# A decoder layer's second feed-forward block: one more seven-product pair per gate and up unit, its column sums loaded instead of added

## The chip, the cores and the metric

The kernel runs on one core of one Trainium2 chip. The metric is device time in microseconds (us) of one execution, the median of several runs. A core has five engines with instruction queues of their own: TensorE (PE) multiplies, VectorE (DVE) and ScalarE (ACT) do element-wise work, GpSimd (POOL) and SyncE (SP) here mostly issue DMAs. Engines wait for each other by semaphores alone, and each works through its own queue in order.

## The reference

One decoder layer on 272 tokens (16 learned meta tokens and 256 real ones) of width 2048, all in float32: a SwiGLU feed-forward block, a mixer (attention and a short convolution, each gated), and a second feed-forward block, all with RMS norms. What matters here is the second block, on the 256 real tokens alone, and the mixer's gates:

```python
D_FF = ((8 * D_MODEL // 3 + 255) // 256) * 256        # 5632

def swiglu_ffn(h, w_gu, w_down):
    gate, up = jnp.split(h @ w_gu, 2, axis=-1)
    return (jax.nn.silu(gate) * up) @ w_down
...
        gates = jax.nn.sigmoid(h @ w_gate[layer]).reshape(Bsz, L, N_BRANCH, D_MODEL)
        merged = jnp.sum(gates * z, axis=2)
        s = s + merged @ w_out[layer]

        h = rms_norm(s, norm_ffn2[layer])
        s = s + 0.5 * swiglu_ffn(h, ffn2_w_gu[layer], ffn2_w_down[layer])
    s = rms_norm(s, norm_final)
    return s[:, N_META:]
```

## The kernel before, in words

**Splitting.** Every float32 weight is used as a high part `wh` (ACT rounds it, L381) and a low part `wl = w - wh` (DVE, L382), activations likewise. A product of two numbers then takes three matmuls: high by high, low by high, high by low (L488 to L490). `parts` (L374) makes `wh` and `wl` of one block of weights, 128 rows by two times 512 columns, into rings of three buffers each. `step` (L239) collects what PE shall do with a block and holds it back until two later blocks are split (`AHEAD`).

**Units.** The gate and up weights of the second block are 11 units of 512 gate and 512 up columns (`thirds`, L975: units 0 to 3, 4 to 7, 8 to 10, each run of units followed by its share of the down projection). Unit 0 goes through `linear_tok`; units 1 to 10 through `gate_up_mix` (L578). The mixer's gates are four more such units (L902). In `linear_mix` (L470) a unit's 2048 rows of weights are eight pairs, a pair being two chunks of 128 rows, and `KINDS` says how each pair is multiplied. Rows in two chunks, tokens in two halves of 128 and columns in gate and up make a 2 by 2 by 2 block product. A pair of kind D multiplies it in eight products of 128x128 by 128x512. A pair of kind S takes seven (Winograd's form): it needs four sums of blocks of activations (made once, L455 to L465) and four sums of blocks of weights, made anew for each pair and unit by DVE (`tt`, L514 to L517: one add of 128x1024, then two of 128x512). An S pair is split in four blocks: one single block of 128x512 (product 3) and three double ones (1 and 2; 6 and 4; 5 and 7). Call the blocks n0 to n3, and a D pair's n0 and n1.

**Buffers.** Loaded weights (`st`) and the sums (`tt`) share a ring of five 8 KB buffers (`ST_BUFS`). The pool "a" has 27 buffers for activations and the like (`N_ACT`).

**End of a unit.** Products are summed in eight PSUM banks. When a bank's last product is done, `done` (L548) brings it into the sums `cgate` and `cup` on ACT and DVE; then comes SiLU on ACT (L582), `up * gate` on DVE (L583), and PE transposes the result in two goes of four (`back`, L589, called from `later` in L498 at pair 2 of the next unit).

**Order.** The framework's scheduler puts each engine's queue in an order of its own when the kernel is built; `issue_after` pins an instruction behind another. SP issues weight loads, POOL issues only eight small loads at the start and two for the last norm.

Of the kernel before, what the change touches and what calls it, by code (L numbers as in the profile page):

```python
# [9 lines left out]
F32 = mybir.dt.float32  # L10
# [5 lines left out]
P = 128  # L16
# [15 lines left out]
W_BUFS = 3  # L32
ST_BUFS = 5
LB = 2
N_ACT = 27
EVICT_AT = 1
# [3 lines left out]
LATER_AT = (4, 6)  # L40
KINDS = "DDDSDSDS"
AHEAD = 2
# [3 lines left out]
def decoder_layer(ctx: ExitStack, tc: tile.TileContext, t, out):  # L46
# [3 lines left out]
    wpool = ctx.enter_context(tc.tile_pool(name="w", bufs=W_BUFS))  # L50
    apool = ctx.enter_context(tc.tile_pool(name="a", bufs=N_ACT))
    tmp = ctx.enter_context(tc.tile_pool(name="tmp", bufs=2))
    psum = ctx.enter_context(tc.tile_pool(name="ps", bufs=8, space=bass.MemoryType.PSUM))
# [184 lines left out]

    def step(use):  # L239

        ahead.append(use)
        drain(AHEAD)

    def drain(n=0):
        while len(ahead) > n:
            ahead.pop(0)()

# [66 lines left out]
    def linear_tok(ops, chunks, k0, name, evict, side_at=(5, 9, 13), hold=0, after=None):  # L314
# [46 lines left out]
        for b, c in enumerate(chunks):  # L361
# [10 lines left out]
            step(lambda b=b, wh=wh, wl=wl: use(b, wh, wl))  # L372

    def parts(src, n=2, held=False):  # L374
# [6 lines left out]
        nc.scalar.copy(out=wh, in_=src)  # L381
        nc.vector.tensor_sub(wl, src, wh.bitcast(F32))  # L382
        return wh, wl
# [46 lines left out]
    class Mixed:  # L430

        def __init__(self, norm, g0):
            self.act, self.sums = Act("hn", 0, SEQ), {}
            self.norm, self.g0 = norm, g0
# [12 lines left out]
        def pair(self, p, f):  # L449
# [4 lines left out]
            nc.vector.tensor_sub(tl[:, :, 1, :], f, tl[:, :, 0, :].bitcast(F32))  # L454
            if KINDS[p] == "S":  # L455
# [5 lines left out]
                nc.vector.tensor_add(q[:, 3, :], a12, q[:, 1, :])  # L461
                sp = apool.tile([P, 4, 2, P], F32R, tag="act", name=f"sp{p}")
                nc.scalar.copy(out=sp[:, :, 0, :], in_=q)
                nc.vector.tensor_sub(sp[:, :, 1, :], q, sp[:, :, 0, :].bitcast(F32))
                self.sums[p] = [[sp[:, k, lo, :] for lo in range(2)] for k in range(4)]  # L465
# [3 lines left out]

    def linear_mix(a, w, cols, name, done):  # L470

# [5 lines left out]

        nd, ns = KINDS.count("D"), KINDS.count("S")
        left = {k: 2 * nd * (k in "234x") + ns * (k != "x") for k in "1234567x"}
# [14 lines left out]
        def use(p, n, products):  # L494

            for k, left_op, wh, wl in products:
                product(k, left_op, wh, wl)
            if p == 2 and later:  # L498
                later.pop(0)()
            if n == (1 if KINDS[p] == "D" else 3):  # L500
                if p == 0:
# [4 lines left out]
        def load(p):  # L506
# [3 lines left out]
            for q in range(2):  # L510
                nc.sync.dma_start(out=st[:, :, q, :], in_=rows[:, :, cols[q] : cols[q] + GW])
            if KINDS[p] == "D":
                return st, None
            tt = wpool.tile([P, 4, GW], F32, tag="st", bufs=ST_BUFS, name="tt")  # L514
            nc.vector.tensor_add(tt[:, 0:2, :], st[:, 0, :, :], st.rearrange("p c q f -> p q c f")[:, 1, :, :])
            nc.vector.tensor_add(tt[:, 2, :], tt[:, 0, :], st[:, 1, 1, :])
            nc.vector.tensor_add(tt[:, 3, :], tt[:, 2, :], st[:, 1, 0, :])  # L517
            return st, tt

        loaded = {0: load(0)}  # L520
        for p, kind in enumerate(KINDS):
            st, tt = loaded[p]
            (a11, a21), (a12, a22) = ([a.block(2 * p + c, i) for i in range(2)] for c in range(2))
# [5 lines left out]
            else:  # L529
# [3 lines left out]
                    (st[:, :, 0, :], (("1", a11, 0), ("2", a12, 1))),  # L533
                    (tt[:, 2:4, :], (("6", s2, 0), ("4", a22, 1))),
                    (tt[:, 0:2, :], (("5", s1, 0), ("7", s3, 1))),
# [8 lines left out]
    def mixed(a, w, cols, name, end):  # L544

# [29 lines left out]

        linear_mix(a, w, cols, name, done)

    def gate_up_mix(a, w_gu, g, m, gi):  # L578
# [7 lines left out]

        mixed(a, w_gu, (g * GW, F + g * GW), "pg", end)

# [254 lines left out]
    yc = Act("yc", NH, SEQ)  # L843
    hg = Mixed(norm2, G_MIX)
    for g in range(2):
# [120 lines left out]
    w_gu, w_down = t["ffn2_w_gu"][0], t["ffn2_w_down"][0]  # L966
    hn = Mixed(norm3, G_FFN2)

# [76 lines left out]
```

## Time and profile before

| what | us |
| --- | --- |
| median of 3 runs (lowest, highest) | 2201.43 (2201.15, 2201.85) |
| the profiled execution: time | 2201.99 |
| the profiled execution: span, first to last instruction | 2200.2 |
| first feed-forward block and mixer, to the last product of `o` | about 1476 |
| second block: unit 0 | 1476 to 1522 |
| second block: units 1 to 10 and the down projections | 1522 to 2200 |

The page tells each engine's busy time, DMA's share in 40 slices, the chain of work that ended last, and groups of instructions by line and operands. The timeline lists single instructions; the windows view sums up a stretch of time. A row's duration is start to end of one instruction; consecutive rows of one engine overlap, so how fast an engine gets on is read from the distance of their starts. A row of PE's weight loads (PEld) belongs to the matmul behind it.

### The profile page before, as it was taken

Reading aid. Unit: us, or ns where it says so; the run is one execution under the profiler, and the core shown is the slowest. Engines: PE = TensorE matmul, PEld = TensorE weight load, DVE = VectorE, ACT = ScalarE, POOL = GpSimd, SP = SyncE. Lnnn points to the kernel's source line nnn. Section 1 sums busy time; section 2 is a strip of 40 time slices with the busy share of each in tenths; the row PEclk is TensorE's granted clock in tenths of the full one; section 3 lists DMA queues with packets and bytes.
Section 4 is the critical chain, followed back from the end, with each engine's and each line's share of the span. In section 5 each row is a group of like instructions: output and inputs, shape, how many; then the busy total and the mean of one; then the engine's idle time right before and its main releaser. Section 6 shows DMA issues by size and latency. Waiting matters only on the chain.

```text
span 2200.2 us, 33207 instructions
## 1 busy us (share of the span) xinstructions
PE 2186.4 (99%) x13534; PEld 1973.3 (90%) x13534; DVE 1467.6 (67%) x1904; ACT 1041.6 (47%) x1301; POOL 6.4 (0%) x17
## 2 busy tenths in 40 slices
PE   9999999999999999999999999999999999999998
PEld 8999999999999999898988888888888888888886
DVE  8555554445555565667897777678886688856985
ACT  6443343334333443444555555455554455534554
POOL 0000000000000000000000000000000000000000
PEclk9999999999999999999999999999999999999999
DMA  7545555555545555444445656554566455665562
GB/s 269 177 173 173 173 173 176 180 178 175 173 172 173 173 176 187 154 138 151 165 153 200 211 193 215 185 187 142 193 224 210 155 201 202 227 211 174 190 229 96
DMA packets 192394, 401.97 MB, mean 183 GB/s; under 512 B 8692, under 2 KB 8880, under 8 KB 192240
## 3 DMA queue, kind: packets, MB, share of 16 engines
q1 hardware_dynamic: 191232, 397.97, 53.1%
q8 instruction: 106, 1.74, 0.3%
q0 software_dynamic: 544, 1.21, 0.2%
q10 hardware_dynamic: 464, 0.66, 0.1%
q14 instruction: 48, 0.39, 0.1%
HBM read 397.71 MB, written 2.10 MB: 182 GB/s over the span
## 4 chain that ended last, share of the span: by engine, by line
PE 98%; DVE 1%; ACT 1%; DMA 0%; issue 0%; SPq 0%; DVEq 0%; ACTq 0%
PE pg L490 5%; PE pg L488 5%; PE pg L489 5%; PE pd L289 4%; PE pu L289 4%; PE pd L287 4%; PE pu L287 4%; PE pu L288 4%; PE pd L288 4%; PE pg L289 4%; PE pg L287 4%; PE pg L288 4%; PE pd L329 4%; PE pd L328 4%; PE pd L327 4%; PE o L285 3%
## 5 line engine op out<-in xcount | busy, mean ns | idle before, releaser
L276 DVE TENSOR_TENSOR wl<-st,wh 128x1024 fp32r<-128x1024 f32 x392 | 478.9, 1224 | 453.5 <-ACT wh L275 452.8
L275 ACT CAST wh<-st 128x1024 fp32r<-128x1024 f32 x392 | 411.3, 1050 | 609.9 <-PE pd L288 146.9
L381 ACT CAST wh<-st 128x1024 fp32r<-128x1024 f32 (+1 forms) x360 | 358.5, 1004 | 366.3 <-PE pd L328 113.8
L382 DVE TENSOR_TENSOR wl<-st,wh 128x1024 fp32r<-128x1024 f32 (+1 forms) x360 | 414.2, 1158 | 130.4 <-ACT wh L381 129.9
L287 PE MATMUL pg<-h,wh 128*128 128x272 f32 x704 | 202.9, 289 | 0.9 <-ACT wh L275 0.8
L287 PE MATMUL pu<-h,wh 128*128 128x272 f32 x704 | 203.1, 289 | 0.0
L289 PE MATMUL pd<-m,wl 128*128 128x272 f32 x704 | 203.0, 288 | 0.0
L289 PE MATMUL pu<-h,wl 128*128 128x272 f32 x704 | 203.0, 288 | 0.0
L287 PE MATMUL pd<-m,wh 128*128 128x272 f32 x704 | 202.9, 288 | 0.0
L288 PE MATMUL pu<-h,wh 128*128 128x272 f32 x704 | 202.4, 288 | 0.0
L288 PE MATMUL pd<-m,wh 128*128 128x272 f32 x704 | 202.4, 287 | 0.0
L288 PE MATMUL pg<-h,wh 128*128 128x272 f32 x704 | 201.7, 287 | 0.0
L289 PE MATMUL pg<-h,wl 128*128 128x272 f32 x704 | 200.6, 289 | 0.9 <-DVE wl L276 0.9
L488 PE MATMUL pg<-wh,hn 128*128 128x512 f32 x390 | 152.7, 391 | 0.0
L489 PE MATMUL pg<-wh,hn 128*128 128x512 f32 x390 | 152.0, 390 | 0.0
L490 PE MATMUL pg<-wl,hn 128*128 128x512 f32 x390 | 151.8, 392 | 0.2 <-DVE wl L382 0.2
L327 PE MATMUL pd<-wh,m 128*128 128x512 f32 x352 | 137.5, 391 | 0.0
L328 PE MATMUL pd<-wh,m 128*128 128x512 f32 x352 | 137.0, 389 | 0.0
L329 PE MATMUL pd<-wl,m 128*128 128x512 f32 x352 | 136.9, 390 | 0.0
L382 DVE TENSOR_TENSOR wl<-tt,wh 128x1024 fp32r<-128x1024 f32 x84 | 101.3, 1222 | 52.8 <-ACT wh L381 42.8
L287 PEld LDWEIGHTS pg<-h,wh 128*128 128x128 f32 x704 | 132.3, 188 | 1.5 <-ACT wh L275 1.5
L288 PEld LDWEIGHTS pg<-h,wh 128*128 128x128 f32 x704 | 132.8, 189 | 0.0
(303 smaller groups left out, 4725.4 us busy)
## 6 DMA issues: line engine op xcount, KB each, us to landing
st<-in_ffn_w_gu_dram SPq DMA_DIRECT2D x184, 512.0 KB, 4.4
st<-in_ffn_w_down_dram SPq DMA_DIRECT2D x88, 1024.0 KB, 5.1
st<-in_ffn_w_gu_dram SPq DMA_DIRECT2D x84, 1024.0 KB, 4.9
st<-in_w_in_dram SPq DMA_DIRECT2D x48, 1024.0 KB, 5.1
st<-in_w_gate_dram SPq DMA_DIRECT2D x64, 512.0 KB, 4.4
st<-in_w_branch_dram SPq DMA_DIRECT2D x32, 512.0 KB, 4.7
st<-in_w_out_dram SPq DMA_DIRECT2D x16, 1024.0 KB, 5.0
xin<-in_x_dram SPq DMA_DIRECT2D x8, 256.0 KB, 8.4
```

The costliest lines, as they stand in the source:

```text
L275: nc.scalar.copy(out=wh[:, :m, :], in_=sw)
L276: nc.vector.tensor_sub(wl[:, :m, :], sw, wh[:, :m, :].bitcast(F32))
L287: nc.tensor.matmul(a, wh[:, i, f], act.part(c, 0, t0, t1), start=first, stop=False)
L288: nc.tensor.matmul(a, wh[:, i, f], act.part(c, 1, t0, t1), start=False, stop=False)
L289: nc.tensor.matmul(a, wl[:, i, f], act.part(c, 0, t0, t1), start=False, stop=last)
L327: nc.tensor.matmul(ps, hi, wh[:, q, :], start=first, stop=False)
L328: nc.tensor.matmul(ps, lo, wh[:, q, :], start=False, stop=False)
L381: nc.scalar.copy(out=wh, in_=src)
L382: nc.vector.tensor_sub(wl, src, wh.bitcast(F32))
L488: nc.tensor.matmul(ps[k], hi, wh, start=first, stop=False)
L489: nc.tensor.matmul(ps[k], lo, wh, start=False, stop=False)
L490: nc.tensor.matmul(ps[k], hi, wl, start=False, stop=left[k] == 0)
```

## The change

`KINDS` becomes two tables. The gates keep their three S pairs (`DDDSDSDS`); the units of the second block get `DDSDSSDS`, four S pairs and four D pairs, so 180 matmuls in place of 183. The transposes of the previous unit are called from pair 1 in place of pair 2 there (`TURN_FFN2`).

In the second block the first two sums of an S pair (`t13`) are no longer added by DVE: POOL issues two DMAs per pair, a plain load and one that adds into what the first wrote, into a pool "aux" of three buffers that takes three buffers from pool "a" and that holds the gates' activation sums before. They are issued up to four pairs ahead. The other two sums (`t24`) stay on DVE, pinned behind the split of a given block (`SUMS_*`). `st` and sums have rings of their own (four buffers of `st`, two of 4 KB for sums), and `st` is loaded two pairs ahead. The single block n0 is split into two 2 KB buffers of pool "tmp" and no longer counts in `AHEAD`.

```diff
-ST_BUFS = 5
+ST_BUFS = 4
-N_ACT = 27
+N_ACT = 24
+N_AUX = 3
-KINDS = "DDDSDSDS"
+KINDS_GATES = "DDDSDSDS"
+KINDS_FFN2 = "DDSDSSDS"
+TURN_GATES = 2
+TURN_FFN2 = 1
+SUMS_GATES = {(2, 1): 3, (4, 1): 5, (6, 1): 7}
+SUMS_FFN2 = {(1, 1): 2, (3, 0): 4, (3, 1): 5, (6, 0): 7}
...
-    def step(use):
-        ahead.append(use)
-        drain(AHEAD)
+    def step(use, ring=True):
+        ahead.append((use, ring))
+        while sum(r for _, r in ahead) > AHEAD:
+            ahead.pop(0)[0]()
...
         wh, wl = (
-            (apool.tile([P, 2, GW], F32R, tag="act", name=nm) if held else wpool.tile([P, 2, GW], F32R, tag=nm, name=nm))
+            tmp.tile([P, 1, GW], F32R, tag="sc", name=nm) if n == 1
+            else (apool.tile([P, 2, GW], F32R, tag="act", name=nm) if held else wpool.tile([P, 2, GW], F32R, tag=nm, name=nm))
...
-                sp = apool.tile([P, 4, 2, P], F32R, tag="act", name=f"sp{p}")
+                sp = (aux if self.in_aux else apool).tile([P, 4, 2, P], F32R, tag="act", name=f"sp{p}")
...
-            if p == 2 and later:
+            if p == a.turn_at and later:
                 later.pop(0)()
...
-            tt = wpool.tile([P, 4, GW], F32, tag="st", bufs=ST_BUFS, name="tt")
-            nc.vector.tensor_add(tt[:, 0:2, :], st[:, 0, :, :], st.rearrange("p c q f -> p q c f")[:, 1, :, :])
-            nc.vector.tensor_add(tt[:, 2, :], tt[:, 0, :], st[:, 1, 1, :])
-            nc.vector.tensor_add(tt[:, 3, :], tt[:, 2, :], st[:, 1, 0, :])
-            return st, tt
+            t13 = t24 = None
+            if kinds[p] == "S":
+                if not fetch:
+                    t13 = wpool.tile([P, 2, GW], F32, tag="tt", bufs=2, name="t13")
+                    nc.vector.tensor_add(t13, st[:, 0, :, :], st.rearrange("p c q f -> p q c f")[:, 1, :, :])
+                t24 = wpool.tile([P, 2, GW], F32, tag="tt", bufs=2, name="t24")
+            return st, t13, t24
+
+        def sum24(k):
+            st, t13, t24 = loaded[k]
+            t13 = fetched.get(k, t13)
+            nc.vector.tensor_add(t24[:, 0, :], t13[:, 0, :], st[:, 1, 1, :])
+            nc.vector.tensor_add(t24[:, 1, :], t24[:, 0, :], st[:, 1, 0, :])
+
+        fetched = {}
+
+        def prefetch(p):
+            t13 = fetched[p] = aux.tile([P, 2, GW], F32, tag="act", name="t13")
+            rows = w[2 * p * P : (2 * p + 2) * P, :].rearrange("(c p) (q f) -> p c q f", p=P, q=2)
+            fs = slice(cols[0], cols[0] + GW)
+            nc.gpsimd.dma_start(out=t13, in_=rows[:, 0, :, fs])
+            nc.gpsimd.dma_start(out=t13, in_=rows[:, :, 1, fs], accum_op=ALU.add)
+
+        far = 2 if fetch else 1
+        loaded = {k: load(k) for k in range(far)}
+        for p, kind in enumerate(kinds):
+            if fetch:
+                for k in range(0 if p == 0 else p + 4, min(p + 5, len(kinds))):
+                    if kinds[k] == "S":
+                        prefetch(k)
...
-                if n == 1 and p + 1 < len(KINDS):
-                    loaded[p + 1] = load(p + 1)
+                if n == 1 and p + far < len(kinds):
+                    loaded[p + far] = load(p + far)
                 wh, wl = parts(src, src.shape[1])
+                if (p, n) in a.sums_at:
+                    with tc.issue_after(split_last[0]):
+                        sum24(a.sums_at[p, n])
...
-                step(lambda p=p, n=n, products=products: use(p, n, products))
+                step(lambda p=p, n=n, products=products: use(p, n, products), src.shape[1] > 1)
...
-        mixed(a, w_gu, (g * GW, F + g * GW), "pg", end)
+        mixed(a, w_gu, (g * GW, F + g * GW), "pg", end, fetch=True)
...
-    hg = Mixed(norm2, G_MIX)
+    hg = Mixed(KINDS_GATES, TURN_GATES, SUMS_GATES, norm2, G_MIX, True)
...
-    hn = Mixed(norm3, G_FFN2)
+    hn = Mixed(KINDS_FFN2, TURN_FFN2, SUMS_FFN2, norm3, G_FFN2, False)
```

What the scheduler makes of it shows in the built queues of a unit whose previous unit was one of the ten as well. On DVE, at the start of such a unit, before (names: `wl<-st` is the split of a block, `pg` a PSUM bank, `cup` and `cgate` the sums at the end of the previous unit):

```order
L565 TENSOR_TENSOR cgate<-pg_17155,u2x 128x512
L567 TENSOR_TENSOR cup<-pg_17312,u2x 128x512
L571 TENSOR_TENSOR cgate<-pg_17316,cgate 128x512
L568 TENSOR_TENSOR cup<-cup,u2x 128x512
L382 TENSOR_TENSOR wl<-st,wh 128x1024
L569 TENSOR_TENSOR cup<-pg_17151,cup 128x512
L572 TENSOR_TENSOR cup<-cup,pg_17316 128x512
L382 TENSOR_TENSOR wl<-st,wh 128x1024
L583 TENSOR_TENSOR cup<-cup,cgate 128x1024
```

and after (line numbers of the changed kernel; L393 is the split, L538 the first add of `t24`, shown as `t`, and L623 the product `up * gate`):

```order
L605 TENSOR_TENSOR cgate<-pg_17259,u2x 128x512
L393 TENSOR_TENSOR wl<-st,wh 128x1024
L607 TENSOR_TENSOR cup<-pg_17384,u2x 128x512
L611 TENSOR_TENSOR cgate<-pg_17388,cgate 128x512
L608 TENSOR_TENSOR cup<-cup,u2x 128x512
L393 TENSOR_TENSOR wl<-st,wh 128x1024
L609 TENSOR_TENSOR cup<-pg_17255,cup 128x512
L612 TENSOR_TENSOR cup<-cup,pg_17388 128x512
L393 TENSOR_TENSOR wl<-st,wh 128x1024
L538 TENSOR_TENSOR t_17589<-t_17568,st 128x512
L623 TENSOR_TENSOR cup<-cup,cgate 128x1024
```

The first add for pair 2 now stands right ahead of the product. A second operation of this size has come in four rows ahead of the first one shown, between the last split of the old unit and the first of the nine operations that end it: the split of pair 2's single block.

On PE the four transposes that read the product stand behind all of pair 1 and the first block of pair 2 before:

```order
L488 MATMUL pgx<-wh,hn_14994 128x512
L489 MATMUL pgx<-wh,hn_14994 128x512
L490 MATMUL pgx<-wl,hn_14994 128x512
L594 MATMUL mt_ps<-ident,cup 128x128 x4
L488 MATMUL pg_17491<-wh,hn_14994 128x512
```

and after in the middle of pair 1's second block (its products into banks 2 and 3 are ahead, 4 and x behind):

```order
L503 MATMUL pg_17616<-wh,hn_14968 128x512
L504 MATMUL pg_17616<-wh,hn_14968 128x512
L505 MATMUL pg_17616<-wl,hn_14968 128x512
L634 MATMUL mt_ps<-ident,cup 128x128 x4
L503 MATMUL pg_17620<-wh,hn_14968 128x512
```

That is 42 matmuls behind the first of the unit; before it was 60.

On POOL, whose queue held nothing at this place, one unit's loads of `t13` now stand thus (pairs 2, 4, 5 and 7; the second of each two adds):

```order
L547 DMA t13_17568<-in_ffn2_w_gu_dram 128x2x512
L548 DMA t13_17568<-in_ffn2_w_gu_dram 128x2x512
L547 DMA t13_17571<-in_ffn2_w_gu_dram 128x2x512
L548 DMA t13_17571<-in_ffn2_w_gu_dram 128x2x512
L547 DMA t13_17605<-in_ffn2_w_gu_dram 128x2x512
L548 DMA t13_17605<-in_ffn2_w_gu_dram 128x2x512
L547 DMA t13_17719<-in_ffn2_w_gu_dram 128x2x512
L548 DMA t13_17719<-in_ffn2_w_gu_dram 128x2x512
```

Each plain load waits for a buffer of "aux", so for DVE's split of the `t13` three before; each adding one waits until the plain one has landed. SP's queue is the same, but that at the start of the kernel the loads of `x` for the second half stand one weight load earlier.

More of the change, by code (lines that the diff above doesn't have):

```diff
@@ L51, in decoder_layer @@
     apool = ctx.enter_context(tc.tile_pool(name="a", bufs=N_ACT))
+    aux = ctx.enter_context(tc.tile_pool(name="aux", bufs=N_AUX))
     tmp = ctx.enter_context(tc.tile_pool(name="tmp", bufs=2))
@@ L237, in decoder_layer, with drain @@
     ahead = []
-    def step(use):
-        ahead.append(use)
-        drain(AHEAD)
-    def drain(n=0):
-        while len(ahead) > n:
-            ahead.pop(0)()
+    def step(use, ring=True):
+        ahead.append((use, ring))
+        while sum(r for _, r in ahead) > AHEAD:
+            ahead.pop(0)[0]()
+    def drain():
+        while ahead:
+            ahead.pop(0)[0]()
     def linear(act, chunks, w, k0, c0, t0, t1, name, evict, before=None, side_at=(5, 9, 13), after=None):
@@ L430, in decoder_layer, with __init__ @@
     class Mixed:
-        def __init__(self, norm, g0):
-            self.act, self.sums = Act("hn", 0, SEQ), {}
+        def __init__(self, kinds, turn_at, sums_at, norm, g0, in_aux):
+            self.kinds, self.turn_at, self.sums_at, self.act, self.sums, self.in_aux = (
+                kinds, turn_at, sums_at, Act("hn", 0, SEQ), {}, in_aux
+            )
             self.norm, self.g0 = norm, g0
@@ L468, in block, with linear_mix @@
             return [self.act.part(c, lo, i * P, (i + 1) * P) for lo in range(2)]
-    def linear_mix(a, w, cols, name, done):
-        nd, ns = KINDS.count("D"), KINDS.count("S")
+    def linear_mix(a, w, cols, name, done, fetch):
+        kinds = a.kinds
+        nd, ns = kinds.count("D"), kinds.count("S")
         left = {k: 2 * nd * (k in "234x") + ns * (k != "x") for k in "1234567x"}
@@ L511, in load @@
                 nc.sync.dma_start(out=st[:, :, q, :], in_=rows[:, :, cols[q] : cols[q] + GW])
-            if KINDS[p] == "D":
-                return st, None
-            tt = wpool.tile([P, 4, GW], F32, tag="st", bufs=ST_BUFS, name="tt")
-            nc.vector.tensor_add(tt[:, 0:2, :], st[:, 0, :, :], st.rearrange("p c q f -> p q c f")[:, 1, :, :])
-            nc.vector.tensor_add(tt[:, 2, :], tt[:, 0, :], st[:, 1, 1, :])
-            nc.vector.tensor_add(tt[:, 3, :], tt[:, 2, :], st[:, 1, 0, :])
-            return st, tt
-        loaded = {0: load(0)}
-        for p, kind in enumerate(KINDS):
-            st, tt = loaded[p]
+            t13 = t24 = None
[24 more added lines that the diff above has]
+                        prefetch(k)
+            st, t13, t24 = loaded[p]
+            t13 = fetched.get(p, t13)
             (a11, a21), (a12, a22) = ([a.block(2 * p + c, i) for i in range(2)] for c in range(2))
@@ L533, in linear_mix, with mixed @@
                     (st[:, :, 0, :], (("1", a11, 0), ("2", a12, 1))),
[L534 to L535 removed]
+                    (t24, (("6", s2, 0), ("4", a22, 1))),
+                    (t13, (("5", s1, 0), ("7", s3, 1))),
                 ]
             for n, (src, products) in enumerate(tiles):
[L538 to L539 removed]
+                if n == 1 and p + far < len(kinds):
+                    loaded[p + far] = load(p + far)
                 wh, wl = parts(src, src.shape[1])
+                if (p, n) in a.sums_at:
+                    with tc.issue_after(split_last[0]):
+                        sum24(a.sums_at[p, n])
                 products = [(k, left_op, wh[:, j, :], wl[:, j, :]) for k, left_op, j in products]
[L542 to L544 removed]
+                step(lambda p=p, n=n, products=products: use(p, n, products), src.shape[1] > 1)
+    def mixed(a, w, cols, name, end, fetch=False):
         ev = {}
@@ L574, in done @@
                 pending.append(lambda: end(gt, up))
-        linear_mix(a, w, cols, name, done)
+        linear_mix(a, w, cols, name, done, fetch)
     def gate_up_mix(a, w_gu, g, m, gi):
```

7 lines of the change are left out of this document (4 added, 3 removed).

## Prediction

> **What bounds the kernel now.** First the page: busy time by engine, and the shares of the chain that ended last.
>
> ```profile
> PE 2186.4 (99%) x13534; PEld 1973.3 (90%) x13534; DVE 1467.6 (67%) x1904; ACT 1041.6 (47%) x1301; POOL 6.4 (0%) x17
> ...
> PE 98%; DVE 1%; ACT 1%; DMA 0%; issue 0%; SPq 0%; DVEq 0%; ACTq 0%
> ```
>
> The chain is PE's own work. Busy time alone would not show that PE runs at its pace, since its rows overlap, so I read the distance of starts. Timeline of PE, unit 5: the first matmul of pair 5 (S), of pair 6 (D) and of pair 7.
>
> ```profile
> 1808.38 0.39 PE L488 MATMUL pg<-wh,sp 128*128 128x512 f32 x1
> ...
> 1813.16 0.39 PE L488 MATMUL pg<-wh,hn 128*128 128x512 f32 x1
> ...
> 1818.61 0.39 PE L488 MATMUL pg<-wh,sp 128*128 128x512 f32 x1
> ```
>
> 21 matmuls take 4.78 us and 24 take 5.45: 0.2275 each in both, so PE waits for nothing inside these pairs. A view of waits says the same for all units of this kind:
>
> ```profile
> PEld pg L490 <- DVE wl L382: 6.1, 24, 0.6
> ```
>
> 24 weight loads waited 6.1 us in all, much of it under the matmul before. So time goes only with matmuls. What stands next in line is read from windows: one steady unit (first matmul of unit 5 to that of unit 6), unit 0, a stretch of the gates, the kernel's start, and two 2 us pieces of it. Columns: length, then busy us (instructions) of PE, weight loads, DVE, ACT and POOL, clock, DMA share, GB/s.
>
> ```profile
> 1780.75:1823.46 42.71, 42.71 (x193) 34.83 (x192) 37.96 (x43) 24.28 (x29) 0.00 (x0) 1.00 0.58 197
> 1476.00:1522.00 46.00, 45.85 (x209) 37.79 (x208) 43.15 (x83) 28.07 (x39) 0.00 (x0) 1.00 0.47 161
> 1155.00:1200.00 45.00, 45.00 (x198) 36.90 (x198) 35.47 (x38) 23.86 (x25) 0.00 (x0) 1.00 0.64 222
> 0.00:50.00 50.00, 45.77 (x333) 43.70 (x334) 40.61 (x89) 32.89 (x54) 5.29 (x15) 1.00 0.83 280
> 12.00:14.00 2.00, 1.47 (x12) 1.25 (x11) 0.38 (x1) 1.46 (x3) 0.00 (x0) 1.00 1.05 405
> 48.00:50.00 2.00, 2.00 (x18) 2.00 (x17) 2.00 (x5) 1.99 (x4) 0.00 (x0) 1.00 1.05 399
> ```
>
> In a unit DVE is the second bound (89% of 42.71), DMA the third (0.58).
>
> **The change, part by part. Matmuls.** Each of ten units turns one D pair into an S pair: 5.45 - 4.78 = 0.67 us of PE, 6.7 in all. This is the whole gain; a unit would take 42.04.
>
> **DVE and ACT, in sum.** Groups of the ten units (mean ns behind the bar):
>
> ```profile
> L515 DVE TENSOR_TENSOR tt<-st 128x1024 f32<-128x1024 f32 x29 | 35.4, 1219 | 8.6 <-DMA st<-in_ffn_w_gu_dram 8.5
> L516 DVE TENSOR_TENSOR tt<-tt,st 128x512 f32<-128x512 f32 x30 | 20.5, 684 | 0.1
> L381 ACT CAST wh<-st 128x512 fp32r<-128x512 f32 x30 | 18.7, 624 | 22.9 <-PE pgx L489 16.6 <-PE pg L489 4.1 <-DVE wl L382 2.1
> L464 DVE TENSOR_TENSOR sp<-sums,sp 128x512 fp32r<-128x512 f32 x1 | 0.7, 686 | 0.0
> L461 DVE TENSOR_TENSOR sums<-hnf,sums 128x128 f32<-128x128 f32 x1 | 0.3, 288 | 0.0
> ```
>
> A unit loses three adds of 128x1024 (to DMA) and gains one split of that size, one single split and two adds of 128x512: -2 x 1.22 + 3 x 0.68 = -0.40, so 37.56 of 42.04 us, 89% as before. ACT gains a double and a single cast (1.05 + 0.62): 25.95 of 42.04. Both still fit. Once, in unit 0, a fourth set of activation sums costs DVE 4 x 0.29 + 0.69 = 1.85 us; DVE has 46.00 - 43.15 = 2.85 idle there. I take nothing; 1.85 if that idle time lies elsewhere.
>
> **The turn moves 18 matmuls forward.** This is the tightest place. DVE's timeline at the end of unit 4, up to the product, then ACT's, then PE's (first matmul of unit 5, and the transposes):
>
> ```profile
> 1778.42 1.23 DVE L382 TENSOR_TENSOR wl<-tt,wh 128x1024 fp32r<-128x1024 f32 x1 [0.20 <-ACT wh L381]
> 1779.56 0.68 DVE L561 TENSOR_TENSOR cgate<-pg,cup 128x512 f32<-128x512 f32 x1
> ...
> 1783.03 0.68 DVE L565 TENSOR_TENSOR cgate<-pg,u2x 128x512 f32<-128x512 f32 x1
> 1783.63 0.68 DVE L567 TENSOR_TENSOR cup<-pg,u2x 128x512 f32<-128x512 f32 x1
> ...
> 1788.89 1.22 DVE L583 TENSOR_TENSOR cup<-cup,cgate 128x1024 f32<-128x1024 f32 x1
> ```
>
> ```profile
> 1775.90 1.05 ACT L381 CAST wh<-tt 128x1024 fp32r<-128x1024 f32 x1 [1.67 <-PE pgx L489]
> ...
> 1777.34 1.05 ACT L381 CAST wh<-tt 128x1024 fp32r<-128x1024 f32 x1
> ```
>
> ```profile
> 1780.75 0.39 PE L488 MATMUL pg<-wh,hn 128*128 128x512 f32 x1
> ...
> 1794.49 0.60 PE L594 MATMUL mt_ps<-ident,cup 128*128 128x128 f32 x4
> ```
>
> The product is ready at 1788.89 + 1.22 = 1790.11, 9.36 after the unit's first matmul; PE asks for it at 13.74. Now PE asks after 42 matmuls: 42 x 0.2275 = 9.56. DVE has two more operations of 128x512 ahead of the product, 0.60 each by the starts of L565 and L567, and it works here without a gap from 1779.56 on. Started at the same moment, the product would come at 9.36 + 1.20 = 10.56, 1.0 too late. But the chain starts earlier. Its first split (1778.42) waited for ACT's cast of 1777.34; that cast's buffer was last used by pair 7's single block, since the single block takes a place in the ring of three. With single blocks out of the ring the cast gets the buffer for which the row of 1775.90 waits: 1.44 earlier. That leaves 10.56 - 1.44 = 9.12, or 0.4 to spare. What is late next are PSUM banks that DVE reads, done on PE's own time. I take nothing. The bounds are 0 and 1.0 us in each of the seven turns of that form (units 1, 2, 4, 5, 6, 8, 9), so 7.0.
>
> **The loads of `t13`.** SP's loads, POOL's two loads for the last norm, and the issue of the first of these:
>
> ```profile
> st<-in_ffn_w_gu_dram SPq DMA_DIRECT2D x184, 512.0 KB, 4.4
> ...
> xin<-in_x_dram SPq DMA_DIRECT2D x8, 256.0 KB, 8.4
> gfin<-in_norm_final_dram POOLq DMA_DIRECT2D x2, 512.0 KB, 5.6
> ```
>
> ```profile
> 1959.46 0.56 POOL L989 DMA_DIRECT2D gfin<-in_norm_final_dram  x1 [1953.20 <-PE pd L329]
> ```
>
> Latency: POOL takes 0.56 per issue and each `t13` is two DMAs in a row, the second waiting for the first: 2 x 5.6 = 11.2 from the row of POOL's queue, 2 x 8.4 = 16.8 at the load of the kernel's start (share 0.83), where `xin` landed in 8.4. Behind a waiting adding load stand POOL's later ones alone. The shortest lead is pair 7's: its buffer comes free with the split of pair 2's last block, its first add stands behind pair 6's first split; between lie pairs 3, 4 and 5 of PE's time, 5.45 + 2 x 4.78 = 15.0. If late, the add holds up DVE with pair 6's second split behind it, which PE wants one block of 12 matmuls (2.7) later: 17.7 in all. Nearest to the POOL row, I take 11.2 and no cost.
>
> Throughput: a unit moves 197 GB/s x 42.71 us = 8.4 MB. Four pairs add 2.1 MB of plain loads and 2.1 MB of adding ones, so 12.6 MB in 42.04 us, 300 GB/s, and 350 if an adding byte costs as two. No row shows an adding load. From below it is a plain load; from above I count its second read as a whole load more. The 2 us windows show 399 and 405 GB/s, so both fit and I take nothing.
>
> The Trainium skill (Collectives: The Full Stack, section "The bandwidth ceiling: the fold count and why AG ≠ RS ≠ AR") puts an add inside a DMA at two reads per byte, with half the rate; no run here shows it, and by it the sum stays as it is. Its page DMA: Bandwidth & Descriptors (Specifications) speaks against the change with about 358 GB/s of HBM per core, which 350 would all but fill; the windows of 399 and 405 exceed it, so the measurement decides.
>
> **Buffers, order, gates.** Four buffers of `st` in place of five: in the first block a buffer lasts 48 matmuls, and 401 matmuls take 50 us:
>
> ```profile
> 100.00:150.00 50.00, 50.00 (x401) 50.00 (x400) 25.76 (x31) 20.29 (x23) 0.00 (x0) 1.00 0.51 175
> st<-in_ffn_w_gu_dram SPq DMA_DIRECT2D x84, 1024.0 KB, 4.9
> ```
>
> 6.0 us per buffer, three in reserve, 4.9 to land: nothing. In the units the ring holds `st` alone, loaded two pairs (over 9 us) ahead of use against 4.4 to land. The same holds at the start, where loads of `x` move up by one weight load. The gates keep their matmuls; for pairs 5 and 7 the second add now stands right ahead of the cast that reads it, so DVE idles one cast, 1.05, twice in a unit, within 45.00 - 35.47 = 9.5 idle per 45 us. Uncovered it would be 8.4 over four units. Pool "a" gives up three buffers to "aux" and with them the gates' three sums: nothing. One stall may go: DVE's first adds (L515 above) waited 8.5 us for loads, and in unit 1 PE paid for one of these. Its timeline there:
>
> ```profile
> 1550.67 0.39 PE L489 MATMUL pg<-wh,hn 128*128 128x512 f32 x1
> 1551.22 0.50 PE L490 MATMUL pg<-wl,hn 128*128 128x512 f32 x1 [0.16 <-DVE wl L382]
> 1551.56 0.39 PE L488 MATMUL pg<-wh,hn 128*128 128x512 f32 x1
> ...
> 1552.48 0.40 PE L489 MATMUL pg<-wh,sp 128*128 128x512 f32 x1
> 1552.95 0.50 PE L490 MATMUL pg<-wl,sp 128*128 128x512 f32 x1
> 1553.29 0.40 PE L488 MATMUL pg<-wh,hn 128*128 128x512 f32 x1
> ```
>
> Two steps take 0.89 and 0.81 where 2 x 0.2275 = 0.455 is the pace: 0.8 lost. Late next would be the casts, so I leave it as the low end.
>
> **Sum.** -6.7. The profiled execution took 2201.99 (span 2200.2, 1.8 around it) and would take 2195.3; the median of the runs lies 0.56 below it, so 2194.7.
>
> **The rivals.** (1) *The product comes late to the turn.* For: 0.4 to spare on a sum of ten durations, DVE without a gap. Against: the ring gives 1.44. A delay of 0.35 to 1.0 us in seven turns gives back 2.4 to 7.0: 2197.1 to 2201.7. (2) *Adding loads slow the DMA engines; slower than before.* One mechanism: if an adding byte costs k plain ones, a unit needs 10.5 + 2.1 k MB; at 399 GB/s that fits 42.04 us up to k = 3.0. From there each further 1 costs 5.3 us in each of ten units, 53 in all; from k = 3.2 the kernel is slower than before, at 3.5 it takes 2221, at 4 some 2248. Against: reads alone give k = 2. For: no row shows such a load. (3) *Pair 7's sums land late.* Beyond 17.7 us each us costs 10; 0.4 to 0.9 us late is 2198.7 to 2203.7. Against: even twice 8.4 stays below. (4) *More goes than matmuls*: unit 1's stall as well, 2193.9.
>
> **How the numbers follow.** Forecast (2193.9 to 2196.5 with small losses) 0.55; rival 1 0.16; rival 2 0.16; rival 3 0.08; rival 4 0.05. The likeliest is 2194.7. Two tenths are about what a measurement of this kernel can tell from no change (0.2% is 4.4 us; faster means below 2197.0, slower above 2205.8). Faster: 0.55 + 0.05 = 0.60. Same: rivals 1 and 3, 0.24. Slower: rival 2, 0.16. A range from 2193.2 (rival 4 less the 0.7 by which the runs shown scatter) to 2203.5 leaves out rival 2 and the last bit of rival 3.
>
> **What would show it.** Right: 180 matmuls in a unit of 42.0 us, no wait of the transposes (L634) for L623, DVE at 37.6 per unit, DMA share below 0.95, `t13` landing in 6 to 8 us. Wrong: PE idle before L634 behind L623 (rival 1); DVE's L538 or ACT's cast waiting for DMA `t13` (3), and with it loads of `st` that land later than 10 us and a DMA share near 1 (2). It is wrong altogether if unit length does not follow the matmul count.

## The result, and the profile after

The changed kernel takes 2219.93 us (median of 6 runs, 2218.36 to 2227.6), the kernel before in the same set 2201.28: a ratio of 1.0093 with an interval of 1.0077 to 1.0109. It is 18.65 us slower, where 6.7 less was forecast, so some 25 us have to be found. The profiled execution took 2218.36, its span 2216.6.

The page of the changed kernel, busy time by engine and the shares of the chain that ended last:

```profile
PE 2183.6 (99%) x13504; PEld 1974.0 (89%) x13504; DVE 1469.3 (66%) x1919; ACT 1058.2 (48%) x1322; POOL 81.5 (4%) x97
...
PE 92%; DMA 4%; DVE 2%; ACT 1%; issue 1%; SPq 0%; DVEq 0%; ACTq 0%
```

The 30 matmuls are gone (13504 against 13534), and PE still shows 99%: the overlapping rows hide what it lost. The chain does not hide it. PE had 98% of it, now 92%, and 4% went to a load. Which load, and who waited for it, is in the views of waits (sum in us, times, longest): PE's first two rows, then the longest rows of ACT and of POOL that name a DMA.

```profile
PE pg L503 <- ACT wh L392: 15.3, 7, 2.8
PE pg L505 <- DVE wl L393: 4.4, 7, 0.7
...
ACT wh L392 <- DMA st<-in_ffn_w_gu_dram: 27.7, 10, 4.1
...
POOL t L548 <- DMA t<-in_ffn_w_gu_dram: 239.5, 40, 9.4
```

L503 to L505 are the three matmuls of a product in the new file, L392 and L393 the cast and the split, L526 the loads of `st`, L547 and L548 the plain and the adding load of `t13`. POOL's row is each adding load waiting for its plain one, as intended. PE waited seven times for a cast, and seven times, right behind it, for a split. There are ten units after unit 0 in runs of three, four and three; seven of them follow another unit directly, and the seven waits stand at these seven passages. One of them, the passage from unit 5 to unit 6, in PE's timeline (start, us, and in brackets the idle time before and what ended it):

```profile
1827.59 0.39 PE L505 MATMUL pg<-wl,sp 128*128 128x512 f32 x1
1829.63 0.50 PE L503 MATMUL pg<-wh,hn 128*128 128x512 f32 x1 [1.66 <-ACT wh L392]
1829.97 0.39 PE L504 MATMUL pg<-wh,hn 128*128 128x512 f32 x1
1830.20 0.40 PE L503 MATMUL pg<-wh,hn 128*128 128x512 f32 x1
1831.26 0.50 PE L505 MATMUL pg<-wl,hn 128*128 128x512 f32 x1 [0.67 <-DVE wl L393]
```

The last matmul of pair 7 starts at 1827.59, the first of the new unit 2.04 later where the pace is 0.2275, and three matmuls on PE stands again, 1.06 from start to start. ACT's timeline over the same time shows why:

```profile
1824.00 0.58 ACT L591 COPY u2x<-pgx 128x512 f32<-128x512 f32 x1
1827.53 0.62 ACT L392 CAST wh<-st 128x512 fp32r<-128x512 f32 x1 [2.95 <-DMA st<-in_ffn_w_gu_dram]
1828.06 0.58 ACT L596 COPY cup<-pg 128x512 f32<-128x512 f32 x1
1828.53 2.94 ACT L392 CAST wh<-st 128x1024 fp32r<-128x1024 f32 x3
```

The cast of 128x512 at 1827.53 is a single block. Pair 7's has long been used; this one belongs to **pair 2 of the next unit**. It stands in ACT's queue ahead of the casts of that unit's pairs 0 and 1 (three of them are the last row), which PE needs first. Nothing holds it back any more: its buffer is no longer one of the ring of three, so it is free early, and the order of the queue, fixed before the run, lets it go first. But its data are not there. The chain of waits (start, us, what) has the load and what it released:

```profile
1818.93 0.37 SPq L526
...
1819.34 8.11 DMA st<-in_ffn_w_gu_dram
...
1827.53 0.63 ACT wh L392
```

The second half of pair 2's load goes out at 1819.34 and takes 8.11 us. ACT was free for the cast at about 1824.6, 5.2 after that issue. Before the change loads of `st` landed in 4.4 us in the median, which would have been in time. Now they take longer; the loads of `st` between 1522 and 2130, before and after (min/median/max):

```profile
DMA to landing us min/median/max: 3.4/4.4/6.5
```

```profile
DMA to landing us min/median/max: 3.4/5.4/11.5
```

The stalls at the seven passages come to 16.4 us over the pace, the gaps behind them to 5.8. After some of them PE is slower for a while. Three windows of the changed kernel, a unit, the first 3.9 us after the stall shown above, and the first 4.6 us after the next stall, from unit 6 to unit 7 (length, busy us of PE, weight loads, DVE, ACT, POOL, clock, DMA share, GB/s):

```profile
1829.63:1875.42 45.79, 42.35 (x189) 34.43 (x189) 37.96 (x44) 25.72 (x30) 7.45 (x8) 1.00 0.91 274
1829.63:1833.50 3.87, 3.20 (x13) 2.35 (x14) 3.87 (x6) 1.94 (x3) 0.00 (x0) 1.00 1.01 248
1875.42:1880.00 4.58, 3.92 (x10) 2.89 (x11) 4.58 (x7) 1.84 (x2) 0.02 (x1) 0.63 1.03 230
```

A unit takes 45.8 us, not 42.0, with DVE at 38.0 and a DMA share of 0.91. In the third window the granted clock is 0.63: matmuls there start 0.427 apart and not 0.2275. In the whole kernel 21 do, 4.2 us more. 16.4, 5.8 and 4.2 are 26.4 us.

### The profile page after: what moved, and what is told of

It is laid out like the page before. It is cut to its first block, busy times and chain, and to the rows that moved or that the text cites. A ratio compares the mean times of both kernels' runs of the same rounds, so it can differ in the third digit from the quotient of the medians.

```text
span 2216.6 us, 33340 instructions
## 1 busy us (share of the span) xinstructions
PE 2183.6 (99%) x13504; PEld 1974.0 (89%) x13504; DVE 1469.3 (66%) x1919; ACT 1058.2 (48%) x1322; POOL 81.5 (4%) x97
## 4 chain that ended last, share of the span: by engine, by line
PE 92%; DMA 4%; DVE 2%; ACT 1%; issue 1%; SPq 0%; DVEq 0%; ACTq 0%
PE pg L505 4%; PE pu L297 4%; PE pd L297 4%; PE pd L295 4%; PE pu L295 4%; PE pu L296 4%; PE pd L296 4%; PE pg L504 4%; PE pg L503 4%; PE pg L297 4%; PE pg L295 4%; PE pg L296 4%; PE pd L337 4%; PE pd L335 4%; PE pd L336 4%; DMA st<-in_ffn_w_gu_dram 4%
## 5 line engine op out<-in xcount | busy, mean ns | idle before, releaser
L393 DVE TENSOR_TENSOR wl<-st,wh 128x1024 fp32r<-128x1024 f32 (+1 forms) x360 | 409.6, 1143 | 145.0 <-ACT wh L392 144.1
L392 ACT CAST wh<-st 128x1024 fp32r<-128x1024 f32 (+1 forms) x360 | 354.5, 991 | 300.1 <-PE pd L336 111.1
L393 DVE TENSOR_TENSOR wl<-t,wh 128x1024 fp32r<-128x1024 f32 x104 | 126.7, 1224 | 62.9 <-ACT wh L392 60.3
L392 ACT CAST wh<-t 128x1024 fp32r<-128x1024 f32 x104 | 108.6, 1051 | 122.9 <-PE pgx L504 76.2
L503 PE MATMUL pg<-wh,hn 128*128 128x512 f32 x360 | 143.3, 398 | 15.3 <-ACT wh L392 15.3
L505 PE MATMUL pg<-wl,hn 128*128 128x512 f32 x360 | 143.5, 399 | 4.4 <-DVE wl L393 4.4
L504 PE MATMUL pg<-wh,hn 128*128 128x512 f32 x360 | 142.3, 395 | 0.0
L295 PEld LDWEIGHTS pg<-h,wh 128*128 128x128 f32 x704 | 132.3, 188 | 1.8 <-ACT wh L283 1.8
```

Of the source, the lines that this page charges most:

```text
L295: nc.tensor.matmul(a, wh[:, i, f], act.part(c, 0, t0, t1), start=first, stop=False)
L393: split_last[0] = nc.vector.tensor_sub(wl, src, wh.bitcast(F32)).ins
L503: nc.tensor.matmul(ps[k], hi, wh, start=first, stop=False)
L504: nc.tensor.matmul(ps[k], lo, wh, start=False, stop=False)
L505: nc.tensor.matmul(ps[k], hi, wl, start=False, stop=left[k] == 0)
```

## The experiments

Theory T has two parts that are both needed: the single block's cast stands early in ACT's queue, some 5 us behind its load's issue (first part), and the adding loads stretch that load past this time (second part). Rival R: the adding loads slow everything, wherever a cast stands. Every ratio below is to the kernel before, run in the same set (2202.3 to 2202.5 us in all of them).

**Only the queue order.** The single block's cast and split are put behind those of the block ahead of it in the program:

```diff
-        nc.scalar.copy(out=wh, in_=src)
-        split_last[0] = nc.vector.tensor_sub(wl, src, wh.bitcast(F32)).ins
+        with ExitStack() as order:
+            if n == 1:
+                order.enter_context(tc.issue_after(copy_last[0]))
+                order.enter_context(tc.issue_after(split_last[0]))
+            copy_last[0] = nc.scalar.copy(out=wh, in_=src).ins
+            split_last[0] = nc.vector.tensor_sub(wl, src, wh.bitcast(F32)).ins
```

> Only the issue order changes: each single-block cast and its split are queued behind those of the block ahead of it, so that in FFN2 the single block of pair 2 is cast behind the four blocks of pairs 0 and 1 and no longer ahead of them. Theory T (ACT's queue stands behind a cast whose load was issued about 5 us before): the seven stalls of 1.8 to 3.2 us between units, the 1 us gaps behind them and the stretches at half clock go, about 25 us; 2193 to 2198 us, and the adding loads still take 178 ns for a packet and st still lands up to 9 to 11 us late. Rival R (the adding loads slow every load, and the matmuls wait for st wherever its cast stands): the stalls move to the cast of pair 0, 1 or 2 and stay; 2212 to 2222 us.

Measured: 2192.64 us (2189.64 to 2193.31), ratio 0.9954 (0.9939 to 0.9969). One edit that removes no load takes 27 us off the change, a little more than T expected, and R falls. The load's landing in this run, same stretch:

```profile
DMA to landing us min/median/max: 3.7/6.5/12.3
```

They land later than in the slow kernel, probably because the units now follow faster, with a DMA share of 0.98 (a window of about one unit's length):

```profile
1786.80:1828.70 41.90, 41.90 (x190) 34.62 (x189) 38.10 (x44) 25.88 (x30) 6.30 (x7) 1.00 0.98 292
```

PE is busy for all of 41.90 us and the clock stays at 1.00. ACT's timeline at one passage:

```profile
1814.08 0.59 ACT L600 COPY cup<-pg 128x512 f32<-128x512 f32 x1
1814.57 1.05 ACT L396 CAST wh<-st 128x1024 fp32r<-128x1024 f32 x1
1815.90 1.06 ACT L396 CAST wh<-st 128x1024 fp32r<-128x1024 f32 x1 [0.28 <-PE pg L508]
1817.26 1.06 ACT L396 CAST wh<-st 128x1024 fp32r<-128x1024 f32 x1 [0.30 <-PE pg L508]
1819.98 1.06 ACT L396 CAST wh<-st 128x1024 fp32r<-128x1024 f32 x1 [1.66 <-PE pgx L508]
1820.94 1.05 ACT L626 ACTIVATE cgate<-cgate 128x1024 f32<-128x1024 f32 x1
1821.90 0.60 ACT L396 CAST wh<-st 128x512 fp32r<-128x512 f32 x1
```

The single block now comes behind the four casts of pairs 0 and 1. Its load went out at 1811.15 and landed at 1821.06, 9.9 us later and 0.84 ahead of the cast. The same load at the place of the change as made would have held ACT for some 7 us.

**The single blocks back in the ring**, as before the change:

```diff
-            tmp.tile([P, 1, GW], F32R, tag="sc", name=nm) if n == 1
-            else (apool.tile(...) if held else wpool.tile(...))
+            (apool.tile(...) if held else wpool.tile(...))
...
-                step(lambda ...: use(p, n, products), src.shape[1] > 1)
+                step(lambda ...: use(p, n, products))
```

> The single blocks go back into the ring of three and count for AHEAD, as before the change; the four S pairs and the adding loads stay. T: the ring holds the cast of pair 2 back as it did before the change, the stalls go; 2193 to 2199 us, within 0.2% of the kernel with the pinned cast. R: 2212 to 2222 us.

Measured: 2194.7 us (2193.04 to 2199.81), ratio 0.9968 (0.9957 to 0.9978). T again: what holds the cast back may be the ring or an edge in the queue. Its median is 2 us above that of the pinned kernel, within the scatter of these runs; what the ring costs comes up again below.

**Without the adding load**, with the early cast and with the pinned one:

```diff
-            nc.gpsimd.dma_start(out=t13, in_=rows[:, :, 1, fs], accum_op=ALU.add)
```

> Leaves out the adding load (t13 holds B11 and B21 alone); everything else, the early cast too, stays. DMA share in the units of FFN2 falls from 0.9 towards 0.6 and st lands in 4.4 to 5 us. R: 2193 to 2197 us. T as two parts (an early cast with a lead of about 5.3 us, and a landing stretched past it): the landing comes back under the lead, so most of the seven stalls go, 2194 to 2200 us. If the early cast alone is enough for the stalls (the lead is too short even for a load in 4.4 us): 2210 to 2219 us.

> Both edits: pinned cast, and no adding load. Both theories: 2192 to 2196 us, the floor of this change, with no PE stall between units over 0.5 us. What this lies below the pinned kernel with the adding loads is what the adding loads cost by themselves: T 0 to 3 us, R 18 to 25 us.

Measured: 2191.54 us (2190.94 to 2196.37) and 2190.61 us (2189.39 to 2191.72), ratios 0.9959 (0.9945 to 0.9973) and 0.9947 (0.9932 to 0.9962). Both medians lie below the ranges expected. The early cast alone does no harm: in the first of the two, ACT's order is that of the change as made at all seven passages. From unit 5 to unit 6 (line numbers one lower for the copies):

```profile
1813.10 0.58 ACT L590 COPY u2x<-pgx 128x512 f32<-128x512 f32 x1
1813.85 0.62 ACT L392 CAST wh<-st 128x512 fp32r<-128x512 f32 x1 [0.17 <-DMA st<-in_ffn_w_gu_dram]
1814.37 0.58 ACT L595 COPY cup<-pg 128x512 f32<-128x512 f32 x1
1814.85 3.08 ACT L392 CAST wh<-st 128x1024 fp32r<-128x1024 f32 x3
```

The load of this single block went out at 1808.43 and landed at 1813.77, after 5.34 us in place of 8.11, and ACT waited 0.17. All loads of `st` in the stretch, and ACT's waits for them (sum in us, times):

```profile
  ACT wh L392: 3.7, 4
...
DMA to landing us min/median/max: 3.6/5.0/8.4
```

ACT still waits for them four times, 3.7 us in all, and by PE's starts that costs 1.0 us in two places. With the cast pinned the adding loads cost about 2 us by the medians, which is T's 0 to 3, and no more than these runs scatter. These two kernels leave out the second half of the sums, so that fewer bytes are moved as well as none added. Whether plain loads of as many bytes would stretch a landing as much was not run.

**How far behind.** The cast is put behind the block four before it (so one block of the new unit is ahead of it), then behind the block three before it (two are ahead):

```diff
+            if n == 1:
+                order.enter_context(tc.issue_after(casts[-4]))    # then casts[-3]
+                order.enter_context(tc.issue_after(splits[-4]))
...
```

> The cast of each single block is queued behind the block four before it: the one of pair 2 stands behind one block of the new unit (1024 wide, a step of about 1.8 us) where the change as made has it ahead of all and the pinned kernel behind four. T: the seven stalls of 1.8 to 3.2 us lose about 1.8 us each and the half clock behind them does not come; 0 to 1.4 us are left at a unit, with the 1 us gap behind it where a stall is left: 2193 to 2206 us. If the stall hung on something else than how long before its load's landing the cast stands, it would stay: 2216 to 2222 us.

> As before, but behind two blocks of the new unit, 3.6 us of lead more than the change as made. T: no stall from this cast is left in most units; 2191 to 2196 us, as with the full pin (2192.6). The other reading (a stall that does not depend on the lead): 2216 to 2222 us.

Measured: 2197.09 us (2194.87 to 2201.57), ratio 0.9977 (0.9967 to 0.9986), and 2191.54 us (2189.26 to 2192.83), ratio 0.9948 (0.9933 to 0.9963). The cost falls with the lead: ACT's wait for `st` is 27.7 us in the change as made, and less behind one block and behind two (one row of each kernel's waits):

```profile
ACT wh L396 <- DMA st<-in_ffn_w_gu_dram: 12.2, 7, 2.5
```

```profile
ACT wh L396 <- DMA st<-in_ffn_w_gu_dram: 4.9, 6, 2.2
```

Behind one block PE paid in another place than expected. The stall between units is gone, but PE waited for the product at the turn, seven times:

```profile
PE mt_ps L639 <- DVE cup L628: 3.6, 7, 0.6
```

That is rival 1 of the prediction, by a delay that it had not named: some 1.7 us of ACT's waiting at each passage use up the 0.4 to spare. From start to start the seven cost 0.69 to 0.99 us each instead of 0.23.

**Three pairs in place of four**, pinned: what the fourth pair is worth.

```diff
-KINDS_FFN2 = "DDSDSSDS"
-SUMS_FFN2 = {(1, 1): 2, (3, 0): 4, (3, 1): 5, (6, 0): 7}
+KINDS_FFN2 = "DDDSDSDS"
+SUMS_FFN2 = {(2, 1): 3, (4, 1): 5, (6, 1): 7}
```

> The pinned kernel with three seven-product pairs for each FFN2 unit, as before the change (24 products for pair 2, no adding load for it, the sums of pairs 3, 5 and 7 after the splits at 2, 4 and 6). The fourth pair is the change's whole gain in the forecast, ten units of three matmuls at 0.2275 us, 6.8 us: 2198.5 to 2201 us if that is right and nothing else in the change moves the time; 2193 to 2196 us if the pinned kernel's 9.9 us below the kernel before come from somewhere else (the loads of st ahead, the shorter DVE).

Measured: 2196.02 us (2195.54 to 2196.8), ratio 0.997 (0.9958 to 0.9982). This is just above the range of the second reading. Against three pairs, the fourth brings 3.4 us (pinned) or 4.5 us (behind two blocks) by the medians. By the spans of the profiled runs it brings 2.4 (2193.7 and 2191.3, pinned) or 6.2 (2187.5, behind two blocks, the fastest run of that kernel): the forecast's 6.7 at most. The other edits, without the fourth pair, are already 6.5 us below the kernel before, where the forecast had nothing.

**The sums on DVE**, four pairs, pinned; then the same without the pin:

```diff
         def sum24(k):
             st, t13, t24 = loaded[k]
-            t13 = fetched.get(k, t13)
+            if fetch:
+                t13 = fetched[k]
+                nc.vector.tensor_add(t13, st[:, 0, :, :], st.rearrange("p c q f -> p q c f")[:, 1, :, :])
...
-            nc.gpsimd.dma_start(out=t13, in_=rows[:, 0, :, fs])
-            nc.gpsimd.dma_start(out=t13, in_=rows[:, :, 1, fs], accum_op=ALU.add)
```

> The pinned kernel with t13 added on DVE at the place of the other sums, no load of t13 on POOL's queue: st lands in 4.4 to 5 us again and DMA share falls to about 0.57. DVE gains four sums of 128x1024 (about 1.2 us each) in a unit: 37.6 to about 42.4 us against 40.0 us of matmuls. If DVE then bounds the units: ten or eleven times 2.4 us, 2212 to 2222 us, and the adding loads are worth their contention. If its sums still hide: 2190 to 2195 us.

> The change as made, its early cast of pair 2's single block too, but t13 added on DVE and no load on POOL's queue. T: the cast stands as early as in the change, but st lands in 4.4 to 5.5 us, inside its lead; no stall over 1 us, 2190 to 2196 us as with the pinned kernel of the same sums (2191.8). If the early cast costs by its place alone (any lead of about 5 us is too short): 2205 to 2219 us.

Measured: 2191.78 us (2191.47 to 2191.95), ratio 0.995 (0.9936 to 0.9965), and 2191.11 us (2190.31 to 2192.19), ratio 0.9949 (0.9936 to 0.9963). The sums hide. A unit of the first of the two:

```profile
1782.62:1824.98 42.36, 42.36 (x192) 35.03 (x191) 41.77 (x48) 25.64 (x29) 0.00 (x0) 1.00 0.61 199
```

DVE is busy for 41.77 of 42.36 us and still PE does not wait. The expectation of 2212 us and more set DVE's 42.4 against 40.0 us of matmuls, and that was too little: 180 at 0.2275 are 40.95, and with the eight transposes of the turn a unit of the pinned kernel takes 41.8. DVE, busy for 98.6% of this window, just fits.

The second run was to settle T's second part on a kernel that computes everything, and does so only in part. Its queues came out in another order: the cast stands as early as in the slow kernel at three of the seven passages, behind one block of the new unit at three, and behind two at one. No two of PE's starts between 1522 and 2130 us lie over 0.45 apart, so it does not stall at any of them. So with no load on POOL's queue the early cast costs nothing at three passages; for all seven the kernel without the adding load has to speak.

**Where the 6.5 us come from.** Three pairs, `t13` on DVE, no loads on POOL's queue (the two edits above together); then also the sums ahead of the splits:

```diff
+                if (p, n) in a.sums_at:
+                    sum24(a.sums_at[p, n])
                 wh, wl = parts(src, src.shape[1])
-                if (p, n) in a.sums_at:
-
-                    with tc.issue_after(split_last[0]):
-                        sum24(a.sums_at[p, n])
```

> The pinned kernel with three pairs, t13 on DVE, no load on POOL's queue. It tells what brought the three pairs with adding loads 6.5 us below the kernel before. Theory G: the sums stand between the splits of earlier pairs instead of ahead of the unit's last splits, so the waits of PE for wl at a unit's end (0.25 us, 32 times before) are gone, whoever adds t13: 2195 to 2198 us. Rival H: DVE's relief by the adding loads did it: 2199 to 2203 us.

> The kernel with three pairs and t13 on DVE (2197.4 us), with the two t24 sums of a pair issued ahead of the split beside which they stand and not queued behind it, on the gates too. Theory G (the place of the sums among the splits is what brings three pairs below the kernel before): PE waits for wl at the ends of units come back, 0.2 to 0.5 us a unit in 14 units: 2200 to 2204 us. If the place of the sums does not matter and the 5 us come from elsewhere (loads further ahead, the single blocks outside the ring, the turn one pair earlier): 2196 to 2199 us.

Measured: 2197.36 us (2196.69 to 2197.98), ratio 0.9976 (0.9966 to 0.9985), and 2197.82 us (2197.3 to 2199.93), ratio 0.998 (0.997 to 0.9989). The first spoke for G, the place of the sums; the second, which moves the sums ahead of the splits and loses nothing, speaks against it. What was left are the single blocks, the loads further ahead and the earlier turn. The kernel before with the single blocks out of the ring and nothing else (the edit of the ring above, the other way), and the three-pair kernel with them back in it:

> The kernel before with one edit: single blocks out of the ring and not counted for AHEAD; sums, loads and pairs as before. If the single blocks bring what three pairs gained with the other edits (5.0 to 6.5 us): 2195.5 to 2199 us. If that comes from the loads further ahead or the sums: 2200.5 to 2203.5 us, no change.

> Three pairs, t13 on DVE, the single blocks back in the ring: e10 (2197.4 us) with that one part undone. Single blocks carry the gain: 2200 to 2203 us. Loads further ahead, or the sums, carry it: 2196.5 to 2199 us.

Measured: 2196.42 us (2195.93 to 2198.31), ratio 0.9975 (0.9963 to 0.9986), and 2199.95 us (2199.32 to 2201.68), ratio 0.9988 (0.9979 to 0.9997). The single blocks alone bring 5.9 us, nearly all of the 6.5. Undone in the three-pair kernel they cost 2.6 of its 5.0, just short of the range expected for that; what the other half hangs on was not run. Set start against start, the same 13534 matmuls in both, the kernel before with its single blocks out of the ring gains 1.7 us in the gates and `z` (1060 to 1390) and 3.3 in the second block (1476 to 2130), unit 1's stall of 0.8 among them. The waits of PE's weight loads for the split go at the same places. The kernel before has, beside the row quoted in the prediction, the first two of these; the kernel before with its single blocks out of the ring has the third in place of all three:

```profile
PEld g L490 <- DVE wl L382: 2.2, 8, 0.4
PEld z L329 <- DVE wl L382: 1.1, 4, 0.3
```

```profile
PEld pg L492 <- DVE wl L384: 0.6, 2, 0.4
```

6.1 + 2.2 + 1.1 = 9.4 us of waits become 0.6. With three pairs and the blocks back in the ring they are back (30 times, then 8, then 4), 8.5 us of waits for 2.6 us of time, so only a part of such a wait is lost time:

```profile
PEld pg L504 <- DVE wl L392: 6.0, 30, 0.3
...
PEld g L504 <- DVE wl L392: 1.4, 8, 0.2
...
PEld z L337 <- DVE wl L392: 1.1, 4, 0.3
```

**The rest that is lost with the cast pinned.** In the first experiment DVE still waited for an adding load, three times:

```profile
DVE t L542 <- DMA t<-in_ffn_w_gu_dram: 7.6, 3, 2.7
```

These are pair 5's sums, whose `t13` waits on POOL's queue for that of pair 4, and PE then stood 0.7 to 1.0 us each time. The cast behind two blocks, and these sums one split later:

```diff
-SUMS_FFN2 = {(1, 1): 2, (3, 0): 4, (3, 1): 5, (6, 0): 7}
+SUMS_FFN2 = {(1, 1): 2, (3, 0): 4, (4, 1): 5, (6, 0): 7}
```

> Adding loads kept, single blocks cast behind two blocks of the new unit, and the sums of pair 5 behind the split at (4, 1) in place of (3, 1). In the pinned kernel DVE waited 2.3 to 2.7 us for pair 5's adding load, three times, and PE then 0.7 to 1.0 us for wl. If that load's lateness is the rest that is lost: no DVE wait for it, 2189 to 2192 us, PE's start gaps at most 18 us in all. If the later sums only move the wait to the cast of t24: 2192 to 2196 us.

Measured: 2190.97 us (2188.86 to 2195.08), ratio 0.9952 (0.9938 to 0.9965). Between 1522 and 2130 us, PE's starts that lie over 0.25 apart come to 2.0 us over the pace, against 4.9 with the pin alone and 30.9 in the change as made. (How the 18 us of the expectation were to be counted is not on record.) DVE waited once, 1.8 us, where no wait was expected, and the sums' waits no longer reach PE. By the medians it cannot be told from the kernel behind two blocks (2191.54) or from the two with the sums on DVE (2191.11, 2191.78). All four beat both kernels, by half a per cent the one before and by 1.3% the change as made. Of them the one without loads on POOL's queue and without a pin differs least from the change, and its DMA share is not near 1.

## Why the prediction was wrong

**The step that failed** stands under "Buffers, order, gates": "In the units the ring holds `st` alone, loaded two pairs (over 9 us) ahead of use against 4.4 to land." It takes no cost for that. Both numbers were wrong for one block. The use was not where the prediction put it: of pair 2, the single block is cast four blocks early, at the end of the unit before, 5.2 us after its load goes out. The prediction followed the freed buffers on DVE, where they let a cast go earlier by 1.44, and did not ask which other cast ACT's queue would now hold ahead of that one. And 4.4 was the landing in a kernel without adding loads; with them it is 5.4 in the median in the change as made (longest 11.5) and 6.5 pinned (longest 12.3). Neither alone comes near such a cost: the order with quick loads gave 2191.54 (without the adding load), and slow loads with the cast behind two blocks or four, or held back by the ring, 2190.97 to 2194.70. Together they cost 27 us, from 2192.64 to 2219.93, of which 16.4 are stalls, 5.8 the gaps behind them, and 4.2 a lower clock.

**"So time goes only with matmuls."** This step missed on the other side. The row of 24 weight loads with 6.1 us of waits was read as mostly hidden, and only about half of it was: the single blocks out of the ring bring 3.3 us of PE's time in the second block, 1.7 in the gates and `z`, and 5.9 by the medians. The prediction saw 0.8 of this, as rival 4. "This is the whole gain" should have been about half of it.

**Matmuls, 6.7 us.** Right in what can be measured: 3.4 to 4.5 us by medians that scatter by some 2 us, 2.4 to 6.2 by spans, and 5.6 for the two kernels with the sums on DVE that differ in nothing else (2197.36 and 2191.78, both pinned).

**DVE and ACT.** Right: 38.10 us of DVE and 25.9 of ACT in 41.90, where 37.56 and 25.95 of 42.04 were forecast. The step was too careful: with all sums on DVE its 41.77 of 42.36 still fitted, so the adding loads, the only source of the loss, buy nothing that these runs can tell.

**The turn.** Right at no cost in the change as made and with the pin, and right that 0.4 us is all there is: with the pin the product ends 0.35 us ahead of the transposes at six of the seven turns, 0.18 at one (in unit 5 the product ends at 1784.22 and the transposes start at 1784.56), and with the cast behind one block the product came late seven times.

**The loads of `t13`, in time.** 6.6 us to land in the change as made, 7.8 pinned, where 5.6 to 8.4 was taken. No pair-7 wait was seen; pair 5's, one of the same kind (rival 3), cost 2.6 us once the stalls were gone. That POOL holds the next pair's adding load behind this one was said in the prediction, and counted for one pair alone.

**The loads of `t13`, in throughput.** In the packet records a 2 KB packet took 84 ns in a load of `st` and 178 in an adding one (medians), so an adding byte costs 2.1 plain ones, near the 2 that the sum took and below the 3.0 from which rival 2 decided. The Trainium skill (Collectives: The Full Stack, "The bandwidth ceiling: the fold count and why AG ≠ RS ≠ AR") says of a collective's add inside a DMA that it needs two source reads and so gets about half the rate, and this agrees. So rival 2 was right on the sign and not on the mechanism: with the cast pinned, a unit's loads still fitted, 292 GB/s at a share of 0.98 without a stall. What its price did not contain is the time that one load takes when the queue of packets is nearly full. The sign to look for that the prediction named, a landing later than 10 us with a DMA share near 1, was met in part: loads of `st` landed in up to 11.5 us, at a share of 0.91, which it had counted among the signs of being right. What waited for them was ACT's early cast of `st`, and not the sums of `t13`.

**Rival 4.** Right as far as it went: unit 1's stall, 0.8 us, is gone in every kernel of this study, but for some 0.25 with the sums on DVE and the pin.

## What to carry to other kernels

When a change gives an instruction a buffer of its own, ask what it will now overtake, read the order on its engine, and look up when its data's load goes out; an instruction that was held back by a buffer may have been held back to advantage. Count a load's lead from its issue to the place where the consumer stands in the queue, and set it against the landing time at the DMA share that the change will bring, not the one it has. And a row of many small waits on an engine that sets the pace is a term of the sum until the starts of that engine show that it is hidden.

## What was not expected of the hardware

The clock dropped after short idle times. Of the seven passages, runs of matmuls at 0.427 us followed those of 2.21, 2.67, 3.16 and 3.17 us from start to start, each with the gap of about 1.05 us three matmuls on; none followed those of 1.79, 2.04 and 2.98, which had the same gap behind them. So their length alone does not decide. The Trainium skill (TensorE: Matmul & The Clock Gate, "What's actually happening") has half rate after at least one idle window of about 3.4 us, in windows that run freely; the dependence on more than the length agrees with that, but a stall of 2.21 us, behind which the clock dropped, is shorter than what it states.

A DMA share of 0.98 over a whole unit of the pinned kernel left PE no wait there, but the median landing of `st` was 6.5 us, not 4.4 as in the kernel before, and the longest 12.3, not 6.5. The issue of an adding load takes POOL 1.18 us, that of a plain one 0.75 (medians of the change as made).
